# A decoder block on one core: gates and first products on GpSimd's queue, one load for keys and queries, operand sums started earlier

## The chip, the cores and the metric

The kernel runs on one core of one Trainium2 chip. The metric is the device time of one execution in microseconds (us), the median of several runs. Engines are called PE (TensorE), DVE (VectorE), ACT (ScalarE), POOL (GpSimd) and SP (SyncE, which only issues transfers here).

## The reference

```python
# x (1, 2048, 1024), all float32; D_RNN = D_ATTN = 1024, 8 heads of 128
shift, scale, gate = adaLN(c)
h = rms_norm(x) * (1 + scale) + shift
# one projection of h by W_in (1024 x 8192), its columns being
# [rnn x | rnn silu-gate | q | k | v | attn silu-gate | merge gate rnn | merge gate attn]
A = rg_lru(causal_depthwise_conv(xr)) * silu(zr)   # recurrent branch -> W -> 1024 columns
B = dilated_attention_mixture(rope(q), rope(k), v) * silu(za)
    # three causal (window, dilation) sets: (128, 1), (512, 4), (2048, 16)
merged = sigmoid(gr) * (A @ W_rnn) + sigmoid(ga) * (B @ W_attn)
out = rms_norm(x + gate * (merged @ W_out))
```

## The kernel before

Every product is fp32 accuracy made of three fp32r matmuls: an operand is split into a high part (ACT, `hi_act`) and a low part (its difference to the high part, DVE or POOL, `lo_dve`, `lo_pool`; their lines are 159, 168 and 165), and `mm3` (line 151) issues high·high, low·high, high·low. A matmul has 128 rows of weights and 512 columns.

The program goes through four stages. First the input projection, in two halves f of 1024 positions (0 to about 690 us, 690 to 1340). It uses a scheme of block products with sums of operands (Strassen's kind): the sums B11, B12, ..., T1 to T4 are made by `build_odd`, a generator that first builds the odd blocks in four steps and then makes their sums in eight half-units (lines 609 to 619), each of five DVE operations and the ACT splits `T<-hx`, `T<-t`. `values_half` interleaves that generator with the products for v (`wide_values`), whose PSUM tiles W, X, V, X, Z ... ACT evicts into `ev` (line 855) and SP stores. `issue_after(last_ev[0])` holds the next two half-units, and all behind them, until the last eviction so far. At the very start `idle_matmuls(n)` and `fill=` put matmuls on a constant (`W<-busy`) between the few real ones.

Then attention, head by head, half f by half f: `load_kq` brings keys and queries of head h and residue c into `kraw` (4 buffers), `split_kq` splits them into KQ. Between the attention's matmuls stand those of the two merged branch projections, as a generator of 64 tiles t ("pj", 24 matmuls each, eight steps k of three). For a tile, `split_y` makes the halves yh, yl of the operand, `load_g` loads the gates (grT for the first 32 tiles; gaT and the first product mrT, made by the first 32, for the rest) into `fg` (4 buffers), `evict` multiplies the product by the gate and adds mrT on DVE (lines 1784, 1786), and `store` writes mrT or the result meT. From tile TAIL0 = 40 on (about 1881.7 us) attention is over and the tiles follow one another; the eviction then writes to a tile `R` of its own rather than into `fg`. Behind tile 63 the output projection of meT, the residual and the last norm end the program.

The order on each engine is the order of the program text, run by generators at fixed steps; the transfers go out in the order of the engine that issues them, and a waiting transfer holds what stands behind it on that engine. In the tail the lines are

```python
if k == 0 and t == TAIL0:
    load_g(t)
if k == 7:
    store(t - 1)
    if t + 1 < len(tiles):
        load_g(t + 1)
```

Of the kernel before, what the change touches and what calls it, by code (L numbers as in the profile page):

```python
# [90 lines left out]
def decoder_block(ctx, tc, x, c, positions, g_norm, w_mod, b_mod, w_in, b_gate, conv_w, conv_b,  # L91
# [12 lines left out]


    vN = scratch("vN", [H, 4, NB * P, P])
    qT = scratch("qT", [D, 4, NB * P])
    kT = scratch("kT", [D, 4, NB * P])
    zaT = scratch("zaT", [D, S])
    grT = scratch("grT", [D, S])  # L110
    gaT = scratch("gaT", [D, S])
# [590 lines left out]
    with tc.manual_schedule():  # L702
        warm = T(vx, [P, 1], F32, "warm", bufs=1)
        nc.scalar.activation(warm[:], ones[:], AF.Sigmoid)
        idle_matmuls(16)
        pc = T(pg, [P, CH], F32, "pg")
        nc.tensor.transpose(pc[:, :KT], prow[:KT, :], ident[:KT, :KT])
        cc = T(vx, [P, KT], F32, "cc")
        nc.vector.tensor_copy(cc[:], pc[:, :KT])
        operand("B11")  # L710
        operand("B21")
        raws = {}
        for j in range(4):
            load_mod(j)
            for k in (2 * j, 2 * j + 1):
                if k < NRAW:
                    raws[k] = load_wide_raw(0, k)
        norm = [T(vx, [P, 3, 2], F32, "ss", bufs=4) for _ in range(2)]

        def squares(i):  # L720
            for n in range(2):
                jk = T(vx, [P, D], BF16, "hf", bufs=2)
                nc.scalar.activation(jk[:], x0[2 * i + n], AF.Square, accum_out=norm[i][:, 0, n : n + 1])

        def scale_act(r):
            nc.scalar.activation(x0[r], x0[r], AF.Copy, scale=norm[r // 2][:, 1, r % 2 : r % 2 + 1])

        def scale_dve(r):
            nc.vector.tensor_scalar(x0[r], x0[r], norm[r // 2][:, 1, r % 2 : r % 2 + 1], None, ALU.mult)

        squares(0)
        nc.scalar.activation(ca[:], cc[:], AF.Sigmoid)
        nc.vector.tensor_tensor(ca[:], ca[:], cc[:], ALU.mult)
        rstd_first(norm[0])
        squares(1)
        idle_matmuls(8)
        pt = T(pg, [P, CH], F32, "pg")
        nc.tensor.transpose(pt[:, :N_PAR], prow[:N_PAR, :], ident[:N_PAR, :N_PAR])
        nc.vector.tensor_copy(par[:], pt[:, :N_PAR])
        rstd_last(norm[0])  # L740
        scale_dve(1)
        sums(0, 1)
        rstd_first(norm[1])
        scale_act(0)
        sums(0, 1)
        rstd_last(norm[1])
        scale_act(2)
        scale_dve(3)
        ws = [wide_tiles() for kh in range(2)]
        even = ("B11", "B21")  # L750

        def products(k, js=range(KH)):
            wide_products(pv0, even, ws[k // KH], (k,), js, first=k == 0, last=k == KT - 1, lows_last=k % 2 == 0)

        def hi_k(k):
            hi_act(ws[k // KH][k % KH // 2][0][:, k % 2], raws[k][:])

        def lo_k(k):
            h, l = ws[k // KH][k % KH // 2]
            lo_dve(l[:, k % 2], raws.pop(k)[:], h[:, k % 2])  # L760
            n = k + NRAW
            if n < KT + KH:
                raws[n] = load_wide_raw(n // KT, n % KT)

        idle_matmuls(6)
        column_sums(0, 0, fill=2)
        hi_k(0)
        sums(0)
        column_sums(0, 1, fill=2)
        lo_k(0)  # L770
        turn_x(0)
        idle_matmuls(2)
        last_sums(0, fill=1)
        modulation(0)
        hi_k(1)
        sums(1, 2)
        build_x(0)
        lo_k(1)
        turn_x(1)
        pv0 = [pj_tile([P, CH]) for j in range(KH)]  # L780
        products(0)
        sums(1, 1)
        build_x(1)
        hi_k(2)
        sums(1, 2)
        lo_k(2)
        sums(1)
        turn_x(2)
        for j in range(1, 4):
            k = 2 * j  # L790
            if j == 2:
                x1 = load_x(hp, 1, "T", 14)
            products(k - 1, (0,))
            for kk in range(2):
                column_sums(j, kk)
            products(k - 1, (1, 2))
            last_sums(j)
            if j < 3:
                sums(j + 1, 1)
            modulation(j)  # L800
            products(k - 1, (3,))
            hi_k(k + 1)
            turn_x(k + 1)
            if j < 3:
                sums(j + 1, 1)
            build_x(k)
            lo_k(k + 1)
            products(k)
            if j < 3:
                hi_k(k + 2)  # L810
                sums(j + 1, 2)
            build_x(k + 1)
            if j < 3:
                sums(j + 1, 1)
                lo_k(k + 2)
                sums(j + 1)
                turn_x(k + 2)
        products(KT - 1)
        ws1 = wide_tiles()
        for k in range(KH):  # L820
            split_wide(ws1, k, raws.pop(KT + k))
# [52 lines left out]
    def values_half(f, xs):  # L874
# [16 lines left out]
        for ws in wide_values(vx, 1, n0, (0, 1), None if f else ws1):  # L891
            next(odd)
        for x, _ in enumerate(wide_values(vx, 1, n1, (1, 0), ws)):
            if x == 0:
                next(odd)
        with tc.issue_after(last_ev[0]):
            next(odd)
            next(odd)
        for x, _ in enumerate(wide_values(vx, 0, n1, (0, 1))):
            next(odd, None)  # L900
            if x == 0:
                next(odd, None)
        assert next(odd, None) is None

    xtail = T(cp, [P, 8, 3], F32, "xtail")
# [214 lines left out]
    plain_at = [None]  # L1120
    pu = [None]
    NT0, NT1 = (4, 5), 3
    QK = ((2 * D, qT, -SCALE), (3 * D, kT, 1.0))

    def scaled(t, ps, u, qs):

# [8 lines left out]

    def rotated_pairs(qp, f, Ct, St):

        for base, dstT, qs in QK:
            def rotated(i, j, ps, u, dstT=dstT, qs=qs):
                n = 2 * f + j  # L1140
                cq = slice(j * CH, (j + 1) * CH)
                t0 = T(qp, [P, CH], F32, "t0", bufs=NT0[f])
# [14 lines left out]
                def store():  # L1157
                    for hh in range(4):
                        r0 = (4 * i + hh) * P
                        nc.sync.dma_start(dstT[r0 : r0 + 32, :, n * P : (n + 1) * P],  # L1160
                                          v[0][hh * 32 : (hh + 1) * 32, :].rearrange("p (r j) -> p r j", r=4))


# [16 lines left out]

    def plain_pairs(f):

        for base, dstT, qs in QK:
            for t in range(0, 6, 2):
                def plain(i, j, ps, u, t=t, dstT=dstT, qs=qs):
                    n = 2 * f + j
                    t0 = plain_at[0]()
                    wait = scaled(t0, ps, u, qs)

                    def store():  # L1190
                        for p0, r0, m in cuts[t + i]:
                            nc.sync.dma_start(dstT[r0 : r0 + m, :, n * P : (n + 1) * P],
                                              t0[p0 : p0 + m, :].rearrange("p (r j) -> p r j", r=4))

                    steps_after(n_prod[0], ((wait + 1, store),))
# [224 lines left out]
    class Head:  # L1420
        def __init__(self, f, h):
            self.f, self.h, self.bk = f, h, banks(f)
            self.nk = (self.bk[1] + 1) * P
            self.Q1, self.V, self.V1, self.u, self.raw = {}, {}, {}, {}, {}


        def load_kq(self, c):
            rows = slice(self.h * P, (self.h + 1) * P)
            t = T(ap_, [P, KQW], F32, "kraw", bufs=4)
            q0 = self.bk[0] * P  # L1430
            queue = nc.scalar if self.f == self.h == 0 and c == 3 else nc.sync
            queue.dma_start(t[:, : self.nk], kT[rows, c, : self.nk])
            queue.dma_start(t[:, self.nk : self.nk + 2 * P], qT[rows, c, q0 : q0 + 2 * P])
            self.raw["kq", c] = t

        def split_kq(self, c):
# [4 lines left out]
        def window_queries(self, i):  # L1441

            t = T(ap_, [P, 2, 4, 4, 32], F32R, "q1")
            for l in range(2):
                src = KQ[:, l, :, self.nk + i * P : self.nk + (i + 1) * P].bitcast(F32)
                copy = nc.gpsimd if self.f or self.h else nc.vector
                copy.tensor_copy(t[:, l], src.rearrange("p r (b a) -> p b r a", b=4))
            self.Q1[i] = t[:].rearrange("p l b r a -> p l b (r a)")
# [45 lines left out]
        def scores_c(self, r):  # L1494
            tiles = []
            for i, n in enumerate(self.bk):
                w = (n + 1) * P
                if self.f or n == 0:
                    ps = T(sc, [P, CH], F32, "sc")
                o0 = P if n == 1 else 0  # L1500
                q = slice(self.nk + i * P, self.nk + (i + 1) * P)
                mm3(ps[:, o0 : o0 + w], KQ[:, 0, r, q], KQ[:, 1, r, q], KQ[:, 0, r, :w], KQ[:, 1, r, :w],
                    first=n != 1, last=True, skip_group_check=True)
                tiles.append((ps[:, o0 : o0 + w], w))

# [8 lines left out]

        def keys(self, l, w0, nb):

            ap = KQ[:, l, 0, w0 * 32 : w0 * 32 + 32]
            return bass.AP(ap.tensor, ap.offset, [list(ap.ap[0]), [32, nb], [KQW, 4], [1, 32]])

        def scores_w(self, i):  # L1520
# [202 lines left out]
    def steps(jobs):  # L1723
# [39 lines left out]
        def split_y(j, k):  # L1763
            if j < len(jobs):
# [1 line left out]
                w, ys, n = jobs[j]  # L1766
                t = Y0.pop((ys is yaT, n, k))
                hi_act(yh[:], t[:])
                (lo_dve if j and k % 2 or j > NB + 1 else lo_pool)(yl[:], t[:], yh[:])

        def load_g(t):
            j, m = tiles[t]
# [2 lines left out]
            G[t] = []  # L1775
            for src in (grT,) if ys is yaT else (gaT, mrT):
                g = T(fl, [P, CH], F32, "fg", bufs=4)
                nc.sync.dma_start(g[:], src[at_])
                G[t].append(g)

        def evict(t, ps):
# [7 lines left out]
        def store(t):  # L1789
            j, m = tiles[t]  # L1790
            w, ys, n = jobs[j]
            nc.sync.dma_start((mrT if ys is yaT else meT)[m * P : (m + 1) * P, n * CH : (n + 1) * CH], G.pop(t)[0][:])

        for k in range(KT):
            split_y(0, k)
# [3 lines left out]
        for t, (j, m) in enumerate(tiles):  # L1799
            ps = T(pj, [P, CH], F32, "pj")  # L1800
            for k in range(KT):
# [18 lines left out]
                else:  # L1820
                    if k == 0 and t == TAIL0:
                        load_g(t)
                    if k == 7:
                        store(t - 1)
                        if t + 1 < len(tiles):
                            load_g(t + 1)
# [375 lines left out]
```

## Time and profile before

| | |
|---|---|
| runs of before (us) | 2179.24, 2180.11, 2183.70; median 2180.11 |
| profiled execution | 2180.94 us, span 2179.2 us |
| busy, share of the span | PE 98%, DVE 68%, ACT 60%, POOL 49% |
| mean granted clock of TensorE | 0.997 |
| bytes moved by DMA | 522.98 MB, mean 240 GB/s |

In the rows of a timeline the first number is the start in us from the start of the span, the second the time that the row takes (matmuls of one kind that follow each other stand in one row; the end of the last is modelled), then engine, line of the kernel, operation, and out<-in by the names of tiles; brackets hold the idle time of the engine before it and what ended it. SPq, ACTq and POOL with DMA_DIRECT2D are issues of transfers. Rows of windows give start:end and length, then the busy time of an engine with its count for each engine asked for, then the granted clock of TensorE, the busy share of the 16 DMA engines and GB/s. In the part of the page on groups a row ends with the idle time before the group and what ended it.

### The profile page before, as it was taken

Reading aid. Unit: us, or ns where it says so; the run is one execution under the profiler, and the core shown is the slowest. Engines: PE = TensorE matmul, PEld = TensorE weight load, DVE = VectorE, ACT = ScalarE, POOL = GpSimd, SP = SyncE. Lnnn points to the kernel's source line nnn. Section 1 sums busy time; section 2 is a strip of 40 time slices with the busy share of each in tenths; the row PEclk is TensorE's granted clock in tenths of the full one; section 3 lists DMA queues with packets and bytes.
Section 4 is the critical chain, followed back from the end, with each engine's and each line's share of the span. In section 5 each row is a group of like instructions: output and inputs, shape, how many; then the busy total and the mean of one; then the engine's idle time right before and its main releaser. Section 6 shows DMA issues by size and latency. Waiting matters only on the chain.

```text
span 2179.2 us, 32758 instructions
## 1 busy us (share of the span) xinstructions
PE 2145.1 (98%) x10564; PEld 1791.9 (82%) x10564; DVE 1483.5 (68%) x2564; ACT 1313.1 (60%) x2621; POOL 1075.2 (49%) x803
## 2 busy tenths in 40 slices
PE   9999999999999999999999999999999999999998
PEld 6878888888788888888888887888888988878886
DVE  6579877868656535545446584577777777688887
ACT  5648668668644537457447532677888887343333
POOL 1357677667666323223224665456666665200543
PEclk9999999999999999999999999999999999999999
DMA  8457887887655378899996666888887877898552
GB/s 302 141 202 255 281 299 270 288 287 240 174 112 164 110 247 284 291 312 310 322 330 214 164 160 194 287 251 253 279 262 222 259 236 239 291 314 296 179 174 107
DMA packets 426608, 522.98 MB, mean 240 GB/s; under 512 B 104166, under 2 KB 291778, under 8 KB 425412
## 3 DMA queue, kind: packets, MB, share of 16 engines
q1 hardware_dynamic: 391860, 421.06, 61.9%
q10 hardware_dynamic: 34384, 99.78, 12.3%
q8 instruction: 84, 1.38, 0.2%
q14 instruction: 88, 0.72, 0.1%
q0 software_dynamic: 192, 0.05, 0.0%
HBM read 332.02 MB, written 188.75 MB: 239 GB/s over the span
## 4 chain that ended last, share of the span: by engine, by line
PE 59%; DMA 6%; issue 2%; POOL 2%; ACT 2%; DVE 2%; SPq 1%; ACTq 0%; POOLq 0%; DVEq 0%
PE X L151 12%; PE V L151 11%; PE pj L151 10%; PE Z L151 6%; PE W L151 6%; PE Y L151 5%; PE o L151 3%; PE sc L151 3%; DMA S<-wD 1%; PE pg L151 1%; DMA kraw<-kT 1%; PE pT L1570 1%; DMA vraw<-vN 1%; PE pT L1583 1%; DMA R<-yaT 1%
## 5 line engine op out<-in xcount | busy, mean ns | idle before, releaser
L165 POOL TENSOR_TENSOR S<-R,S 128x512 fp32r<-128x512 f32 x192 | 293.2, 1535 | 182.6 <-ACT S L159 89.3
L151 PE MATMUL X<-T,S 128*128 128x512 f32 x1344 | 326.2, 392 | 4.7 <-ACT ev L855 3.6
L151 PE MATMUL pj<-yh,S 128*128 128x512 f32 x896 | 324.5, 403 | 2.3 <-DMA S<-wD 1.6
L151 PE MATMUL V<-T,S 128*128 128x512 f32 x1344 | 324.2, 390 | 0.2 <-DVE ev L454 0.2
L151 PEld LDWEIGHTS X<-T,S 128*128 128x128 f32 x1344 | 253.3, 189 | 59.2 <-ACT ev L855 4.0
L151 PEld LDWEIGHTS V<-T,S 128*128 128x128 f32 x1344 | 252.0, 188 | 53.8 <-DVE ev L454 0.7
L165 POOL TENSOR_TENSOR S<-s,S 128x512 fp32r<-128x512 f32 x116 | 172.2, 1484 | 144.9 <-ACT S L159 105.5
L151 PEld LDWEIGHTS pj<-yh,S 128*128 128x128 f32 x896 | 168.4, 188 | 32.6 <-DVE st L1485 2.0
L151 PE MATMUL pj<-yl,S 128*128 128x512 f32 x448 | 176.2, 393 | 1.9 <-POOL yl L165 1.4
L1486 ACT ACTIVATE pp<-pp,st 128x256 f32<-128x256 f32 (+3 forms) x256 | 133.5, 523 | 52.9 <-DVE st L1485 52.3
L159 ACT ACTIVATE S<-s 128x512 fp32r<-128x512 f32 x124 | 77.4, 624 | 142.7 <-DVE s L284 92.0
L151 PE MATMUL Z<-T,S 128*128 128x512 f32 x672 | 162.0, 390 | 0.0
L151 PE MATMUL Y<-T,S 128*128 128x512 f32 x672 | 161.8, 390 | 0.0
L151 PE MATMUL W<-T,S 128*128 128x512 f32 x672 | 161.6, 389 | 0.0
L159 ACT ACTIVATE S<-R 128x512 fp32r<-128x512 f32 x200 | 121.2, 621 | 60.1 <-issue 20.4
L168 DVE TENSOR_TENSOR ptl<-pT,pth 128x384 fp32r<-128x384 f32 (+1 forms) x160 | 97.8, 628 | 77.3 <-ACT pth L159 75.1
L151 PEld LDWEIGHTS W<-T,S 128*128 128x128 f32 x672 | 126.0, 188 | 26.9 <-issue 0.9
L151 PEld LDWEIGHTS Z<-T,S 128*128 128x128 f32 x672 | 126.1, 188 | 26.2
L151 PEld LDWEIGHTS Y<-T,S 128*128 128x128 f32 x672 | 125.9, 188 | 26.1
L974 DVE SCALAR_TENSOR_TENSOR xc<-xr,par,xc 128x512 f32<-128x512 f32 x96 | 103.6, 1079 | 54.9 <-ACT xc L968 52.7
L165 POOL TENSOR_TENSOR s<-R,s 128x512 fp32r<-128x512 f32 x32 | 44.1, 1378 | 187.8 <-ACT s L159 168.7
L1550 ACT ACTIVATE pp<-pp,M 128x256 f32<-128x256 f32 (+3 forms) x256 | 118.0, 523 | 9.6 <-DVE M L1673 9.6
(417 smaller groups left out, 4902.9 us busy)
## 6 DMA issues: line engine op xcount, KB each, us to landing
sD<-S ACTq DMA_DIRECT2D x140, 512.0 KB, 3.6
S<-sD SPq DMA_DIRECT2D x140, 512.0 KB, 5.0
S<-wD SPq DMA_DIRECT2D x82, 512.0 KB, 5.6
R<-in_w_in_dram SPq DMA_DIRECT2D x144, 256.0 KB, 3.6
wD<-s ACTq DMA_DIRECT2D x64, 256.0 KB, 5.1
T<-in_w_mod_dram SPq DMA_DIRECT2D x16, 512.0 KB, 8.9
vN<-ev SPq DMA_DIRECT2D x32, 256.0 KB, 2.7
zaT<-ev SPq DMA_DIRECT2D x32, 256.0 KB, 4.4
```

The lines of the kernel that those rows point to most:

```text
L151: nc.tensor.matmul(o, lhsT=l, rhs=r, start=st, stop=sp, **kw)
L159: nc.scalar.activation(o, i, AF.Copy)
L165: nc.gpsimd.tensor_tensor(o, i, h.bitcast(F32), ALU.subtract)
L168: return nc.vector.tensor_tensor(o, i, h.bitcast(F32), ALU.subtract).ins
L974: nc.vector.scalar_tensor_tensor(xc, xr[:, i : i + CH], cw(i), xc, ALU.mult, ALU.add)
L1486: nc.scalar.activation(pdst, pdst, AF.Exp, bias=m_, scale=-1.0, accum_out=l_)
L1550: nc.scalar.activation(pp, pp, AF.Copy, scale=w)
L1570: nc.tensor.transpose(pt[:, c0 + j * P : c0 + (j + 1) * P], pp[i][:, k * P : (k + 1) * P], ident)
L1583: nc.tensor.transpose(pt[:, c * P : (c + 1) * P], pp[:, half * P : (half + 1) * P], ident)
```

## The change

It has five parts.

1. Keys and queries share one scratch tensor kqT, laid out so that a head's keys and queries for one half f lie next to each other; `load_kq` issues one transfer instead of two. For the first head three of the four go out on ACT's queue (before, one did).
2. At the start two and three idle matmuls and one fill more.
3. `values_half` calls the generator of the operand sums four times, where it called it once, while the tiles of the odd bank's first products run, and once per step after `issue_after` instead of twice first.
4. For the first tiles' operand, yl of k = 6 and 7 is made by DVE, not POOL.
5. From tile 40 on the gates and first products are loaded on POOL's queue, the results from tile 39 on are stored on it too, and both happen at step k = 2 instead of k = 7.

```diff
-    qT = scratch("qT", [D, 4, NB * P])
-    kT = scratch("kT", [D, 4, NB * P])
+    kqT = scratch("kqT", [D, 4, 2 * NB * P])
+    q_column = lambda n: (n if n < 2 else NB + n) * P
+    k_column = lambda n: (2 + n) * P
...
         turn_x(0)
-        idle_matmuls(2)
-        last_sums(0, fill=1)
+        idle_matmuls(4)
+        last_sums(0, fill=2)
...
         turn_x(1)
+        idle_matmuls(3)
...
         for x, _ in enumerate(wide_values(vx, 1, n1, (1, 0), ws)):
-            if x == 0:
+            for _ in range((1, 2, 1, 0)[x]):
                 next(odd)
         with tc.issue_after(last_ev[0]):
             next(odd)
             next(odd)
-        for x, _ in enumerate(wide_values(vx, 0, n1, (0, 1))):
+        for _ in wide_values(vx, 0, n1, (0, 1)):
             next(odd, None)
-            if x == 0:
-                next(odd, None)
...
+            self.q0, self.k0 = (self.nk, 0) if f else (0, 2 * P)
...
-            q0 = self.bk[0] * P
-            queue = nc.scalar if self.f == self.h == 0 and c == 3 else nc.sync
-            queue.dma_start(t[:, : self.nk], kT[rows, c, : self.nk])
-            queue.dma_start(t[:, self.nk : self.nk + 2 * P], qT[rows, c, q0 : q0 + 2 * P])
+            c0, w = self.f * 2 * P, self.nk + 2 * P
+            (nc.scalar if self.f == self.h == 0 and c else nc.sync).dma_start(t[:, :w], kqT[rows, c, c0 : c0 + w])
...
-                (lo_dve if j and k % 2 or j > NB + 1 else lo_pool)(yl[:], t[:], yh[:])
+                (lo_dve if (k % 2 if j else k > 5) or j > NB + 1 else lo_pool)(yl[:], t[:], yh[:])
...
-                nc.sync.dma_start(g[:], src[at_])
+                (nc.gpsimd if t >= TAIL0 else nc.sync).dma_start(g[:], src[at_])
...
-            nc.sync.dma_start((mrT if ys is yaT else meT)[...], G.pop(t)[0][:])
+            (nc.gpsimd if t >= TAIL0 - 1 else nc.sync).dma_start((mrT if ys is yaT else meT)[...], G.pop(t)[0][:])
...
-                    if k == 7:
+                    if k == 2:
                         store(t - 1)
                         if t + 1 < len(tiles):
                             load_g(t + 1)
```

The queries and keys that the attention reads out of KQ move with the offsets q0 and k0; nothing else of it changes. Three places show how instructions move. Line numbers of the changed kernel are up to two higher or lower.

The first is ACT's order at the end of the first half's products for v: `ev` are the last four evictions, `T` splits of operand sums, `S` splits of weights. Before:

```order
L159 ACTIVATE T_894<-t_197_1115 128x512
L159 ACTIVATE S_228_1262<-R_218_1236 128x512
L159 ACTIVATE S_226_1256<-s_219_1238 128x512
L855 ACTIVATE ev_1178<-W_1024 128x512
L159 ACTIVATE T_888<-hx_687 128x512
L855 ACTIVATE ev_1187<-X_1025 128x512
L159 ACTIVATE T_890<-hx_691 128x512
L855 ACTIVATE ev_1196<-V_1026 128x512
L855 ACTIVATE ev_1205<-X_1027 128x512
L159 ACTIVATE T_894<-t_211_1211 128x512
```

And in the changed kernel:

```order
L160 ACTIVATE T_902<-t_200_1139 128x512
L279 DMA sD<-S_223_1254 128x1024
L160 ACTIVATE S_229_1270<-R_219_1244 128x512
L160 ACTIVATE S_227_1264<-s_220_1246 128x512
L857 ACTIVATE ev_1194<-W_1056 128x512
L857 ACTIVATE ev_1203<-X_1057 128x512
L857 ACTIVATE ev_1212<-V_1058 128x512
L857 ACTIVATE ev_1221<-X_1059 128x512
L160 ACTIVATE S_231_1290<-R_218_1242 128x512
```

All splits T of this stage now stand ahead of the four evictions, which follow one another.

The second is SP's order at the start of attention, with the loads of the first head (`kraw`), of weights (`S<-wD`) and of a gate. Before:

```order
L1432 DMA kraw_12128<-kT 128x256
L1433 DMA kraw_12128<-qT 128x256
L1432 DMA kraw_12131<-kT 128x256
L1433 DMA kraw_12131<-qT 128x256
L1432 DMA kraw_12134<-kT 128x256
L1433 DMA kraw_12134<-qT 128x256
L339 DMA S_2258_12149<-wD 128x1024
L339 DMA S_2260_12168<-wD 128x1024
```

And in the changed kernel:

```order
L1395 DMA msk_12088<-in_cst_dram 128x896
L1432 DMA kraw_12136<-kqT 128x512
L340 DMA S_2259_12153<-wD 128x1024
L340 DMA S_2261_12172<-wD 128x1024
L1778 DMA fg_12183<-grT 128x512
```

Five issues have left SP's queue ahead of the weights; three are on ACT's.

The third is POOL's order where the tail begins, at tile 40. Before:

```order
L1687 TENSOR_TENSOR zt_19118<-zt_19118,yw_19284 128x2x256
L165 TENSOR_TENSOR yl_19530<-R_3766_19363,yh_19529 128x512
L165 TENSOR_TENSOR yl_19550<-R_3783_19451,yh_19549 128x512
L165 TENSOR_TENSOR yl_19586<-kraw_19066,yh_19585 128x512
L165 TENSOR_TENSOR st_4003_20731<-s_4002_20720,st_4003_20731 128x512
```

And in the changed kernel:

```order
L1687 TENSOR_TENSOR zt_19062<-zt_19062,yw_19228 128x2x256
L1778 DMA fg_19501<-gaT 128x512
L166 TENSOR_TENSOR yl_19474<-R_3767_19307,yh_19473 128x512
L166 TENSOR_TENSOR yl_19494<-R_3784_19395,yh_19493 128x512
L1778 DMA fg_19503<-mrT 128x512
L1792 DMA meT<-fg_19430 128x512
L1778 DMA fg_19520<-gaT 128x512
L1778 DMA fg_19522<-mrT 128x512
L166 TENSOR_TENSOR yl_19535<-kraw_19010,yh_19534 128x512
L1792 DMA meT<-R_3832_19572 128x512
```

Four transfers now stand between the second and the third yl of tile 40's operand, and three for each tile follow.

More of the change, by code (lines that the diff above doesn't have):

```diff
@@ L1122, in decoder_block @@
     NT0, NT1 = (4, 5), 3
-    QK = ((2 * D, qT, -SCALE), (3 * D, kT, 1.0))
+    QK = ((2 * D, q_column, -SCALE), (3 * D, k_column, 1.0))
     def scaled(t, ps, u, qs):
@@ L1136, in rotated_pairs, with rotated @@
     def rotated_pairs(qp, f, Ct, St):
-        for base, dstT, qs in QK:
-            def rotated(i, j, ps, u, dstT=dstT, qs=qs):
+        for base, column, qs in QK:
+            def rotated(i, j, ps, u, column=column, qs=qs):
                 n = 2 * f + j
@@ L1159, in store @@
                         r0 = (4 * i + hh) * P
-                        nc.sync.dma_start(dstT[r0 : r0 + 32, :, n * P : (n + 1) * P],
+                        nc.sync.dma_start(kqT[r0 : r0 + 32, :, column(n) : column(n) + P],
                                           v[0][hh * 32 : (hh + 1) * 32, :].rearrange("p (r j) -> p r j", r=4))
@@ L1181, in plain_pairs, with plain @@
     def plain_pairs(f):
-        for base, dstT, qs in QK:
+        for base, column, qs in QK:
             for t in range(0, 6, 2):
-                def plain(i, j, ps, u, t=t, dstT=dstT, qs=qs):
+                def plain(i, j, ps, u, t=t, column=column, qs=qs):
                     n = 2 * f + j
@@ L1191, in store @@
                         for p0, r0, m in cuts[t + i]:
-                            nc.sync.dma_start(dstT[r0 : r0 + m, :, n * P : (n + 1) * P],
+                            nc.sync.dma_start(kqT[r0 : r0 + m, :, column(n) : column(n) + P],
                                               t0[p0 : p0 + m, :].rearrange("p (r j) -> p r j", r=4))
@@ L1444, in window_queries @@
             for l in range(2):
-                src = KQ[:, l, :, self.nk + i * P : self.nk + (i + 1) * P].bitcast(F32)
+                src = KQ[:, l, :, self.q0 + i * P : self.q0 + (i + 1) * P].bitcast(F32)
                 copy = nc.gpsimd if self.f or self.h else nc.vector
@@ L1500, in scores_c @@
                 o0 = P if n == 1 else 0
-                q = slice(self.nk + i * P, self.nk + (i + 1) * P)
-                mm3(ps[:, o0 : o0 + w], KQ[:, 0, r, q], KQ[:, 1, r, q], KQ[:, 0, r, :w], KQ[:, 1, r, :w],
+                q = slice(self.q0 + i * P, self.q0 + (i + 1) * P)
+                ks = slice(self.k0, self.k0 + w)
+                mm3(ps[:, o0 : o0 + w], KQ[:, 0, r, q], KQ[:, 1, r, q], KQ[:, 0, r, ks], KQ[:, 1, r, ks],
                     first=n != 1, last=True, skip_group_check=True)
@@ L1515, in keys @@
         def keys(self, l, w0, nb):
-            ap = KQ[:, l, 0, w0 * 32 : w0 * 32 + 32]
+            ap = KQ[:, l, 0, self.k0 + w0 * 32 : self.k0 + w0 * 32 + 32]
             return bass.AP(ap.tensor, ap.offset, [list(ap.ap[0]), [32, nb], [KQW, 4], [1, 32]])
@@ L1791, in store @@
             w, ys, n = jobs[j]
-            nc.sync.dma_start((mrT if ys is yaT else meT)[m * P : (m + 1) * P, n * CH : (n + 1) * CH], G.pop(t)[0][:])
+            (nc.gpsimd if t >= TAIL0 - 1 else nc.sync).dma_start((mrT if ys is yaT else meT)[m * P : (m + 1) * P, n * CH : (n + 1) * CH], G.pop(t)[0][:])
         for k in range(KT):
```

## The prediction

> **What bounds the kernel now.** I read the page first, then TensorE's timeline at every place where its matmuls do not follow each other, then the engine that each of these stalls names.
>
> ```profile
> span 2179.2 us, 32758 instructions
> PE 2145.1 (98%) x10564; PEld 1791.9 (82%) x10564; DVE 1483.5 (68%) x2564; ACT 1313.1 (60%) x2621; POOL 1075.2 (49%) x803
> 0.00:50.00 50.00, 46.48 (x238) 0.97 0.94 320
> 100.00:150.00 50.00, 46.41 (x194) 0.93 0.63 199
> 1300.00:1936.00 636.00, 621.32 (x3781) 1.00 0.80 253
> 1936.00:2168.00 232.00, 232.00 (x1026) 1.00 0.61 205
> ```
>
> TensorE (PE) works 98% of the span, so a change can win only where it stands idle or runs at a lower clock. The windows (length, PE's busy time, granted clock, share of the DMA engines) say where that is: 3.5 us in the first 50, 3.6 us and a clock of 0.93 around 128 us, 14.7 us in attention and the start of the tail, nothing in the last 232 us. The change has a part at each of the first three places. The profiled execution took 2180.94 us, the median of the runs is 2180.11: I add my sum to the median; the profiled execution lies 0.83 us above it.
>
> **Operand sums moved ahead (around 128 us).** TensorE's, then ScalarE's (ACT), then VectorE's (DVE) timeline:
>
> ```profile
> 122.67 1.52 PE L151 MATMUL X<-S,T 128*128 128x512 f32 x6
> 127.77 5.49 PE L151 MATMUL X<-T,S 128*128 128x512 f32 x12 [3.59 <-ACT ev L855]
> 126.40:129.80 3.40, 2.03 (x5) 1.65 (x6) 3.37 (x3) 2.23 (x4) 2.98 (x2) 0.50 0.41 129
> 129.80:133.20 3.40, 3.40 (x10) 2.63 (x9) 2.50 (x5) 1.71 (x4) 0.00 (x0) 0.50 0.45 147
> 124.57 0.57 ACT L855 ACTIVATE ev<-W 128x512 f32<-128x512 f32 x1
> 126.60 0.63 ACT L159 ACTIVATE T<-hx 128x512 fp32r<-128x512 f32 x1 [1.46 <-DVE hx L612]
> 127.14 0.58 ACT L855 ACTIVATE ev<-X 128x512 f32<-128x512 f32 x1
> 105.67 0.69 DVE L168 TENSOR_TENSOR T<-hx,T 128x512 fp32r<-128x512 f32 x1 [19.04 <-ACT T L159]
> 117.93 1.78 DVE L612 TENSOR_TENSOR hx<-hx,T 128x512 f32<-128x512 f32 x1
> ```
>
> Six matmuls start 1.36 us apart in a steady row (122.67 to where the next would start, 124.03), that is 0.227 us each. So TensorE lost 127.77 − 124.03 = 3.74 us waiting for ACT's eviction ev<-X, and then had half the clock (0.50) in both windows: the twelve matmuls took from 127.77 to about 133.06, 5.3 us in place of 12 × 0.227 = 2.7, another 2.6. Together 6.3 us. ACT was late because the split T<-hx stands ahead of that eviction and waits for DVE's operand sums; DVE had stood idle for 19.04 us before 105.67 for the code holds two of these half-units, and with them all behind, until after the last eviction of the tiles before. The change starts three of the eight half-units ahead of that point, fifteen DVE operations and their ACT splits, at 0.69 us each some 10 us of DVE's work that now lies in its 19 us of idle time; on ACT the last four evictions stand together with no split between. I estimate the eviction at about 122.2 (DVE's chain ends some 5 us sooner), before 124.03. Stall and half clock go: **−6.3**. Bounds: −3 if the sums come only so much sooner that the wait, but not the clock, is halved; −6.5. What is late next in this stage is the second ev<-X, which waits for a store to free its buffer; TensorE needs that bank two tiles (5.4 us) later. In the second half of the projections the same code has a small cover, and I put half a microsecond there on the other side: **+0.4**, by no row.
>
> **The start.** Seven more idle matmuls and one more filler are meant for the clock.
>
> ```profile
> 20.00:24.00 4.00, 4.00 (x11) 0.57 1.08 362
> 38.26 0.63 ACT L159 ACTIVATE S<-R 128x512 fp32r<-128x512 f32 x1 [4.74 <-DMA R<-in_w_in_dram]
> ```
>
> At half clock eight matmuls took 0.427 in place of 0.227 us, 1.6 us. But the DMA engines are full there (1.08), and ACT still waits 4.74 us for a weight at 38.26: time won at 22 us is waited for at 38. **−0.3**, bounds −1.3 and +0.2 (one more filler in a row that ends on the sums).
>
> **Start of attention.** Here stands a stall of each kind that two parts of the change touch:
>
> ```profile
> 1347.62 5.04 POOL L165 TENSOR_TENSOR yl<-T,yh 128x512 fp32r<-128x512 f32 x4
> 1351.47 0.50 PE L151 MATMUL pj<-yl,S 128*128 128x512 f32 x1 [0.27 <-POOL yl L165]
> 1352.71 0.50 PE L151 MATMUL pj<-yl,S 128*128 128x512 f32 x1 [0.28 <-POOL yl L165]
> 1358.14 0.85 PE L151 MATMUL sc<-kq 128*128 128x128 f32 x5 [0.40 <-DVE kq L168]
> 1361.97 0.47 PE L151 MATMUL pj<-yh,S 128*128 128x512 f32 x1 [1.59 <-DMA S<-wD]
> 1352.68 0.32 SPq L1432 DMA_DIRECT2D kraw<-kT  x1
> 1356.36 0.80 SPq L339 DMA_DIRECT2D S<-wD  x2
> ```
>
> GpSimd (POOL) makes the low parts yl of the first tile one after another, 1.26 us each, and TensorE catches up with it; the load of the second kraw waits until 1352.68 for a tile that POOL's last yl frees, and the weights S<-wD stand behind it on SP, issued at 1356.36, landed after TensorE wanted them. Now the last two low parts are DVE's, which is idle here, head 0's other loads are on ACT's queue, which has nothing to do for 10 us, and the weight loads stand right behind the first kraw. The idle times are 0.27 + 0.28 + 0.40 + 1.59 = 2.5 us; counted from start to start, as above, 3.4. **−3.4**, bounds −1.5 (the weights still late) and −3.6. In the rest of attention 63 issues fewer on SP: I take **−0.8**, bounds −3 and +1, since stalls there name DVE and POOL, not SP.
>
> **First tail steps: the gates.**
>
> ```profile
> 1890.35 0.50 PE L151 MATMUL pj<-yh,S 128*128 128x512 f32 x1 [0.69 <-ACT S L159]
> 1910.88 0.73 PE L151 MATMUL pj<-yh,st 128*128 128x512 f32 x2 [0.44 <-DVE st L168]
> 1928.83 0.73 PE L151 MATMUL pj<-yh,st 128*128 128x512 f32 x2 [1.35 <-DVE st L168]
> 1934.37 0.50 PE L151 MATMUL pj<-yl,st 128*128 128x512 f32 x1 [0.71 <-DVE yl L168]
> 1925.35 0.69 DVE L1784 TENSOR_TENSOR R<-pj,fg 128x512 f32<-128x512 f32 x1 [2.19 <-DMA fg<-gaT]
> 1926.88 0.69 DVE L1786 TENSOR_TENSOR R<-R,fg 128x512 f32<-128x512 f32 x1 [0.84 <-DMA fg<-mrT]
> ```
>
> DVE waits 2.19 + 0.84 us for two gates, and 2 us later TensorE waits 1.35 us for a split that stands behind them on DVE. The four stalls of this stretch are 0.69 + 0.44 + 1.35 + 0.71 = 3.2 us idle, 3.85 from start to start. Gates issued five steps (5 × 0.68 = 3.4 us) sooner cover 2.19 + 0.84. **−3.3**, bounds −1.5 and −3.85.
>
> **The new wait.** The stores and gates are now in POOL's order, and a low part that TensorE needs stands behind them:
>
> ```profile
> 1881.37 1.30 POOL L165 TENSOR_TENSOR yl<-kraw,yh 128x512 fp32r<-128x512 f32 x1
> 1882.86 0.69 DVE L1786 TENSOR_TENSOR fg<-fg,fg 128x512 f32<-128x512 f32 x1
> 1883.58 0.32 SPq L1778 DMA_DIRECT2D fg<-mrT  x1
> 1887.55 0.74 SPq L1792 DMA_DIRECT2D meT<-fg  x1
> 1891.65 0.32 SPq L1778 DMA_DIRECT2D fg<-mrT  x1
> 1886.32 0.39 PE L151 MATMUL pj<-yl,S 128*128 128x512 f32 x1
> 1.30 0.71 POOL L642 DMA_DIRECT2D prow<-in_b_mod_dram  x1 [0.46 <-issue]
> 4.03 0.52 POOL L642 DMA_DIRECT2D prow<-in_lam_dram  x1
> L165 POOL TENSOR_TENSOR st<-s,st 128x512 fp32r<-128x512 f32 x8 | 11.3, 1416 | 134.8 <-ACT st L159 134.8
> DMA to landing us min/median/max: 2.8/5.2/10.9
> ```
>
> Before, POOL made this yl at 1881.37, and TensorE used it at 1886.32, 5 us later. Now four transfers stand ahead of it: mrT of tile 40, free only after the eviction of tile 39 (1882.86 + 0.69 = 1883.55; SP issued it at 1883.58), the store of tile 39, gaT of tile 41, and mrT of tile 41, whose buffer is the source of that store. On SP this last one waited from the store at 1887.55 to 1891.65, 4.1 us. So on POOL: 1883.58, an issue of 0.7, the store from 1884.3, landed at 1888.4, the last issue 0.65, the yl 1.30, ready at 1890.35: TensorE waits 1890.35 − 1886.32 = 4.0 us. An issue of 0.65 is an estimate between the rows of 0.52 and 0.71 us, for shorter transfers. As that is longer than the 3.74 us that cost half the clock at 128 us, I add the same 2.6: **+6.6**. Bounds from the landing times of meT: 2.8 gives a stall of 2.7 without the clock, 10.9 gives 10.8 + 2.6 = 13.4. The Trainium skill ("TensorE: Matmul & The Clock Gate", What's actually happening) has the clock halved after an idle window of about 3.4 us that runs freely, so a stall of 4.0 holds a whole window only if it starts at the right moment; by that rule the sum would have +4.0 here in most phases. The trace has half clock after 3.59 us of idle time and none after 1.59, which agrees.
>
> In the steady tail POOL is all but idle (the last row: from 1935 us on, 134.8 us before eight operations); three issues of 0.65 are 2 us in a tile of 24 × 0.227 = 5.45, and gates issued by 3.8 us after a tile's start land 5.2 later, at 9.0, needed at 11.2. Nothing for that.
>
> The sum: −6.3 + 0.4 − 0.3 − 3.4 − 0.8 − 3.3 + 6.6 = **−7.1**: 2180.11 − 7.1 = **2173.0**.
>
> **Rivals.**
> *The new wait is short* (no half clock, landing 2.8 to 4.1): 2.6 to 3.9 us less, 2169.1 to 2170.4. For it: the row of landings; against: the same wait took 4.1 on SP. 16%.
> *The stall at 128 us stays or goes elsewhere*, DVE's chain being slowed (its 128x512 operations take 1.78 us there when POOL works too), or the new wait has the longest landing: 2173.0 + 6.3 = 2179.3, or 2173.0 + 6.8 = 2179.8, no difference that can be told. 22%.
> *POOL's issues are slow, and the gates fall behind.* No row shows POOL issuing a transfer of 128 rows beside a busy DVE. The point from which it decides is 5.45 / 3 = 1.8 us an issue, beyond which three no longer fit in a tile; at 2.0 each of 23 tiles takes 0.55 us more, 12.7 us: 2185.7, slower; at 3.0 it would be 2255. Against: rows of 0.52 to 0.71 and DVE's tail work, whose operations of 0.68 us show no contention. The Trainium skill ("SBUF — State Buffer", two separate sides) warns that GpSimd cannot write its descriptors while DVE runs certain copies, and says that operations of two inputs are not among them; no run here shows it. 12%. Both this far end of the new wait and the stall at 128 us left in place: 2186.1, 5%.
>
> **How the numbers follow.** Forecast 45%. Some 0.2% (4.4 us) is what a measurement can tell from no change. Faster by more: 45 + 16 = 61%; same: 22%; slower: 12 + 5 = 17%. The range reaches from 2167.5 (the short wait, and the other gains at their far bounds) to 2181.5 (the second rival and the noise of the median); it leaves out the slower cases.
>
> **What would show it.** Right: no PE stall on ACT ev at 128 us and a clock of 1.00 there; S<-wD issued before 1354; no DVE wait on fg beyond 0.5 us after 1900; one PE wait on POOL yl of about 4 us near 1880, with half clock behind it. Wrong: POOL issues above 1 us, PE waits spread over the tail, or the wait at 128 us turned over to DVE.

## The result, and the profile after

The changed kernel took 2188.58 us (median, 2187.92 to 2190.71) against 2180.26 before: a ratio of 1.0038 (1.0027 to 1.0049), 8.3 us slower, where 7.1 faster was forecast. The page and the windows of its profile:

```profile
span 2186.8 us, 32665 instructions
PE 2146.7 (98%) x10571; PEld 1792.1 (82%) x10571; DVE 1486.6 (68%) x2566; ACT 1311.8 (60%) x2621; POOL 1112.4 (51%) x874
0.00:50.00 50.00, 46.62 (x245) 1.00 0.94 320
100.00:150.00 50.00, 49.64 (x218) 1.00 0.64 202
1300.00:1936.00 636.00, 615.47 (x3747) 0.99 0.79 249
```

The stage at 128 us is mended (49.64 busy and full clock, against 46.41 and 0.93). The window of attention and the tail's start is worse: 20.5 us without a matmul where there were 14.7. To compare stages I use one measure, worked out from all matmuls of a profile: from the start of each to the start of the next, less what that takes in a steady row (0.227 us for 512 columns, less for narrower ones). Half clock is in it. In us:

| stage (us from the start) | before | after | forecast of the change | measured |
|---|---|---|---|---|
| 0 to 50 | 8.0 | 6.4, and seven more matmuls of 0.227 | −0.3 | 0.0 |
| 100 to 150 (operand sums) | 6.5 | 0.7 | −6.3 | −5.8 |
| 150 to 450 | 1.1 | 4.7 | none | +3.6 |
| 550 to 800 | 3.4 | 3.8 | +0.4 | +0.4 |
| 1300 to 1400 (start of attention) | 5.6 | 8.2 | −3.4 | +2.6 |
| 1400 to 1850 | 22.6 | 22.3 | −0.8 | −0.3 |
| 1850 to 2000 (tail) | 4.9 | 12.0 | −3.3 + 6.6 | +7.1 |

The last column adds up to 7.6 us, the difference of the two spans. Nearly all of the tail's loss is one wait. GpSimd's (POOL's) timeline, then TensorE's (PE's) row, then SP's rows:

```profile
1883.95 0.56 POOL L1778 DMA_DIRECT2D fg<-mrT  x1 [2.18 <-DVE fg L1786]
1884.51 0.54 POOL L1792 DMA_DIRECT2D meT<-fg  x1
1887.51 0.54 POOL L1778 DMA_DIRECT2D fg<-gaT  x1 [2.45 <-DMA meT<-fg]
1892.53 0.54 POOL L1778 DMA_DIRECT2D fg<-mrT  x1 [4.48 <-DMA meT<-fg]
1893.08 1.27 POOL L166 TENSOR_TENSOR yl<-kraw,yh 128x512 fp32r<-128x512 f32 x1
1894.41 0.79 PE L152 MATMUL pj<-yl,S 128*128 128x512 f32 x1 [8.29 <-POOL yl L166]
1879.53 1.08 SPq L1792 DMA_DIRECT2D meT<-fg  x1
1883.24 0.67 SPq L1928 DMA_DIRECT2D st<-in_w_o_dram  x1
```

The chain is the forecast's: mrT of tile 40, the store of tile 39, gaT and mrT of tile 41, then the yl that TensorE waits for. But gaT waited until 1887.51 for the store of tile 38 that SP had issued at 1879.53, 8.0 us; and the last mrT until 1892.53 for the store issued at 1884.51, again 8.0 us (the profile puts its landing 7.7 us after the issue). From start to start TensorE lost 8.45 us, and 1.9 us more at half clock until 1898.5.

At the start of attention TensorE's, ACT's and SP's rows say what took the place of the four stalls before:

```profile
1349.22 0.50 PE L152 MATMUL pj<-yl,S 128*128 128x512 f32 x1 [0.69 <-POOL yl L166]
1358.53 0.50 PE L152 MATMUL pj<-yh,S 128*128 128x512 f32 x1 [0.67 <-DVE fg L1784]
1361.64 2.45 PE L152 MATMUL sc<-kq,q 128*128 128x128 f32 x12 [2.14 <-DVE q L1446]
1349.20 1.92 ACTq L1432 DMA_DIRECT2D kraw<-kqT  x3
1359.80 0.63 ACT L160 ACTIVATE kq<-kraw 128x512 fp32r<-128x512 f32 x1 [0.85 <-DMA kraw<-kqT]
1348.60 3.11 SPq L340 DMA_DIRECT2D S<-wD  x2
1352.00:1358.00 6.00, 5.75 (x28) 4.33 (x26) 1.52 (x3) 1.26 (x2) 0.00 (x0) 1.00 1.02 395
```

The weights S<-wD, which TensorE had waited for, go out at 1348.60, ahead of three of the first head's loads (1349.20). In the window behind it the DMA engines are full (1.02, 395 GB/s). So the weights are there, and the last part of keys and queries is split only at 1359.80, after which DVE makes q and TensorE has waited 2.14 us.

### The profile page after: what moved, and what is told of

Its sections match the earlier page's. It is cut to its first block, busy times and chain, and to the rows that moved or that the text cites. A ratio compares the mean times of both kernels' runs of the same rounds, so it can differ in the third digit from the quotient of the medians.

```text
span 2186.8 us, 32665 instructions
## 1 busy us (share of the span) xinstructions
PE 2146.7 (98%) x10571; PEld 1792.1 (82%) x10571; DVE 1486.6 (68%) x2566; ACT 1311.8 (60%) x2621; POOL 1112.4 (51%) x874
## 3 DMA queue, kind: packets, MB, share of 16 engines
q10 hardware_dynamic: 34528, 100.30, 12.3%
## 4 chain that ended last, share of the span: by engine, by line
PE 55%; DMA 7%; POOL 4%; DVE 3%; issue 3%; ACT 1%; SPq 1%; ACTq 0%; POOLq 0%; DVEq 0%
PE X L152 11%; PE V L152 11%; PE pj L152 8%; PE Z L152 6%; PE W L152 6%; PE Y L152 5%; PE o L152 3%; PE sc L152 3%; POOL kq L166 1%; DMA vraw<-vN 1%; PE pg L152 1%; PE pT L1570 1%; DMA kraw<-kqT 1%; POOL yl L166 1%; DMA fg<-gaT 1%
```

## The experiments

All ratios are to the kernel before, run beside it on the same chip. Stages are given by the measure above. My theory after the result: the loss is the one wait on GpSimd's order, plus the order of loads at the start of attention; the rivals are named in each expectation.

**e1, part 5 alone.** The kernel before with the two queues and the step of the tail:

```diff
-                nc.sync.dma_start(g[:], src[at_])
+                (nc.gpsimd if t >= TAIL0 else nc.sync).dma_start(g[:], src[at_])
...
-            nc.sync.dma_start((mrT if ys is yaT else meT)[...], G.pop(t)[0][:])
+            (nc.gpsimd if t >= TAIL0 - 1 else nc.sync).dma_start((mrT if ys is yaT else meT)[...], G.pop(t)[0][:])
...
-                    if k == 7:
+                    if k == 2:
                         store(t - 1)
```

> The kernel before with part 5 alone (gates, first products and stores of the tail on GpSimd's queue, at step k = 2). Theory (the yl of k = 6 in tile 40 stands on GpSimd behind two transfers that wait for stores to land): one TensorE wait of 8 us or more on POOL yl near 1890 and about 2 us of half clock, less the 3 to 4 us of small DVE waits in tiles 40 to 49 that go: 2180.3 + 8.4 + 2 - 3.5 = 2187. Rival A (the loss of the whole change comes from the start of attention and the stage behind 150 us): no slower than before, 2177 to 2181. Rival B (GpSimd's issues cost more in every tile): a loss spread over the tail, no single wait above 3 us.

2188.36 us, 1.0040 (1.0027 to 1.0053). One wait of 8.12 us on yl, tail 12.3 us. This part alone loses all that the change loses.

**e2, the change without part 5** (the same edit, taken back).

> The changed kernel with part 5 undone (all on SP at k = 7 again). Theory: the wait on POOL yl is gone, the rest of the change remains: at the operand sums -5.8 and +3.6 given back behind 150 us, at the start of attention +2.6, small things +0.3: 2180.3 + 0.7 = 2181, so no difference from before. Rival A: the other four parts lose on their own, 2184 or more. The forecast's own terms without the new wait and without the gates: 2180.3 - 10.4 = 2170.

2179.60 us, 0.9997 (0.9989 to 1.0006): no difference. The tail is at 3.9. The other four parts together bring nothing.

**e3, tile 40's transfers after the low part**: the changed kernel with one number in one tile.

```diff
-                    if k == 2:
+                    if k == (5 if t == TAIL0 else 2):
                         store(t - 1)
```

> The changed kernel with one step moved: in tile 40 alone the store of tile 39 and the gates of tile 41 are issued at k = 5 instead of k = 2, so that GpSimd makes the yl of k = 6 ahead of them. Theory: the one long wait goes, 8.4 us and 2 us of clock, and the rest of the tail keeps its gain: 2188.6 - 10.4 = 2178, at most 2180 if tile 41's gates are now late. Rival B (GpSimd's issues cost in every tile): gains at most 3, 2185 or more.

2179.95 us, 0.9997 (0.9988 to 1.0006), 8.6 us less than the changed kernel from one number in one tile. The tail is at 3.0. GpSimd's issues in every tile cost nothing that shows.

**e4, part 3 alone**: before, with `values_half` of the change.

```diff
-            if x == 0:
+            for _ in range((1, 2, 1, 0)[x]):
                 next(odd)
...
-        for x, _ in enumerate(wide_values(vx, 0, n1, (0, 1))):
+        for _ in wide_values(vx, 0, n1, (0, 1)):
             next(odd, None)
-            if x == 0:
-                next(odd, None)
```

> The kernel before with part 3 alone (operand sums started earlier). Theory: the wait and the half clock at 128 us go, -5.8, and 3.6 is given back between 150 and 250 us because the later work of ACT and GpSimd does not move with TensorE: 2178. Rival (the loss behind 150 us belongs to another part, the start): -5.8 in full, 2174.5.

2177.76 us, 0.9988 (0.9980 to 0.9997). The stage at 128 us goes from 6.5 to 0.5, the one from 150 to 450 stands at 3.6. Part 3 pays, about 2.5 us. The rival falls: the start is as before here, and the stage behind 150 us is still above the 1.1 of before.

**e5, part 1 alone**: before, with `kqT` and

```diff
+            (nc.scalar if self.f == self.h == 0 and c else nc.sync).dma_start(t[:, :w], kqT[rows, c, c0 : c0 + w])
```

> The kernel before with part 1 alone (one load for keys and queries, three of the first head's four on ACT's queue). Theory (at the start of attention the DMA engines are full, and the weights S<-wD, which now stand ahead of the first head's loads, land first, so that the keys and queries land later): the wait of 1.8 us for the weights goes, a wait of TensorE of 2 to 4 us for kq or q of the first head comes in its place: excess between 1300 and 1400 of 7 to 9 us against 5.6 before, 2180.3 + 2 = 2182. The forecast: the same excess 2 to 3 us lower, 2178.

2183.45 us, 1.0016 (1.0008 to 1.0025). The start of attention is at 8.8, with the wait that the changed kernel shows. TensorE's timeline:

```profile
1362.11 0.50 PE L152 MATMUL pj<-yh,S 128*128 128x512 f32 x1 [0.96 <-DVE fg L1785]
1365.23 1.78 PE L152 MATMUL sc<-kq,q 128*128 128x128 f32 x12 [2.15 <-DVE q L1447]
```

**e6, part 4 alone.**

```diff
-                (lo_dve if j and k % 2 or j > NB + 1 else lo_pool)(yl[:], t[:], yh[:])
+                (lo_dve if (k % 2 if j else k > 5) or j > NB + 1 else lo_pool)(yl[:], t[:], yh[:])
```

> The kernel before with part 4 alone (yl of k = 6 and 7 of the first tile on DVE). Theory: the tile that holds up the second kraw load is free 2 us sooner, the loads and the weights behind them on SP go out sooner in the same order as before: the two waits on POOL yl go or turn into one (DVE and GpSimd slow each other: 1.70 and 1.25 us an operation in the changed kernel), excess between 1300 and 1400 of 3.5 to 5, 2179. Rival (part 4 is what spoils the start of attention): 7 or more, 2182.

2180.32 us, 1.0001 (0.9992 to 1.0009): neutral, start of attention at 4.8. The move saves less than two operations: beside DVE's two, GpSimd's two take 3.43 us together, 1.72 each, where all four took it 5.04, 1.26 each. (Of the two figures in the expectation, 1.70 is GpSimd's and 1.25 DVE's.)

**e7, the step alone**: before, with `k == 2` in place of `k == 7`, all on SP.

> The kernel before with the tail's store and gates at step k = 2, but still on SP's queue. Theory (it is GpSimd's order that carries the wait to TensorE; on SP the same waits for stores to land, 8 us and more, hold only loads of weights): no wait on POOL yl; the weights S<-wR and st behind it come later, which may cost 0 to 3 us: 2180 to 2183. Rival (the step alone does it): 2186 or more.

2186.11 us, 1.0028 (1.0018 to 1.0038). My theory was wrong here: without GpSimd's queue the step still loses 6 us. There is no wait on yl, but SP's, DVE's and TensorE's rows show that the early transfers now hold up something else:

```profile
1886.51 0.43 SPq L1792 DMA_DIRECT2D meT<-fg  x1
1892.35 0.32 SPq L1778 DMA_DIRECT2D fg<-mrT  x1
1893.67 0.42 SPq L2137 DMA_DIRECT2D st<-gateD  x1
1891.64 0.68 DVE L1784 TENSOR_TENSOR R<-pj,fg 128x512 f32<-128x512 f32 x1
1900.22 1.29 DVE L1932 TENSOR_TENSOR st<-st,st 128x512 f32<-128x512 f32 x2 [5.97 <-DMA st<-gateD]
1902.26 0.47 PE L151 MATMUL pj<-yh,S 128*128 128x512 f32 x1 [2.49 <-DVE R L1784]
```

The load of mrT for tile 41 holds SP until 1892.35. The profile names what ended this wait: not a store, but DVE's eviction of tile 40 (R, done at 1892.32). The loads for the output projection stand behind it: gateD goes out at 1893.67 (1886.80 before), DVE waits 5.97 us for it and, being in order, evicts the next tile late. So the early step costs some 6 us on either queue. On GpSimd the landing of a store comes into the path, on SP an eviction; the queue decides what is waited for and who pays.

**e8, e3 with the first head's loads back on SP, ahead of the weights.**

```diff
-            (nc.scalar if self.f == self.h == 0 and c else nc.sync).dma_start(...)
+            (nc.scalar if self.f == self.h == 0 and c == 3 else nc.sync).dma_start(...)
```

> The kernel of e3 with the first head's loads of c = 1 and 2 back on SP, ahead of the weights as before (one load each, yl of k = 6 and 7 on DVE). Theory: the keys and queries land first again, excess between 1300 and 1400 falls from 8.5 to 4 or 5: 2179.9 - 4 = 2176. Rival (it is the single, longer load that is slow, not its place): no change, 2180.

2176.08 us, 0.9981 (0.9972 to 0.9989): the time that was expected, 3.9 us less than e3. The profiles do not show it in one place: the start of attention fell only from 8.5 to 6.9; the tail fell from 3.0 to 0.8 and the stage behind 150 us from 5.7 to 3.9, which this edit does not touch. A single profile of a stage scatters by about 2 us. ACT's and TensorE's rows:

```profile
1355.62 0.63 ACT L160 ACTIVATE kq<-kraw 128x512 fp32r<-128x512 f32 x1 [10.09 <-DMA kraw<-kqT]
1356.97 1.82 ACT L160 ACTIVATE kq<-kraw 128x512 fp32r<-128x512 f32 x3 [0.73 <-DMA kraw<-kqT]
1356.30 0.33 PE L152 MATMUL sc<-kq 128*128 128x128 f32 x1 [1.25 <-ACT kq L160]
```

All four parts are now split by 1358.8 and the wait for q is gone, but the first comes later, and TensorE waits for that.

**e9, the changed kernel without mrT for tile 41** (its result lacks that addend).

```diff
-            for src in (grT,) if ys is yaT else (gaT, mrT):
+            for src in (grT,) if ys is yaT else (gaT,) if t == TAIL0 + 1 else (gaT, mrT):
```

> The changed kernel without the load of the first product (mrT) for tile 41 alone, and without its addition (that tile's result lacks it). GpSimd's order then has one transfer less ahead of the yl of k = 6, the one that waited until 1892.53 for the store of tile 39. Theory (the wait is the landing of stores, one after the other): the yl is made when gaT of tile 41 is out, at 1888.05 + 1.27 = 1889.3; TensorE waits 3.4 us instead of 8.4, about 2188.4 - 5 = 2183, 2181.5 if the half clock goes too. Rival (GpSimd's issues or its queue are slow as such): the wait shrinks by one issue, 0.6 us.

2181.56 us, 1.0009 (1.0000 to 1.0018); the wait, in TensorE's timeline:

```profile
1887.32 0.50 PE L152 MATMUL pj<-yl,S 128*128 128x512 f32 x1 [3.66 <-POOL yl L166]
```

3.8 us from start to start instead of 8.45: leaving out one issue of 0.54 us takes 4.6 us from the wait. It is the landing that the transfer waits for. The half clock behind the wait stays.

**e10, part 2 alone.**

```diff
-        idle_matmuls(2)
-        last_sums(0, fill=1)
+        idle_matmuls(4)
+        last_sums(0, fill=2)
...
         turn_x(1)
+        idle_matmuls(3)
```

> The kernel before with part 2 alone (seven idle matmuls and a fill more at the start). Theory: clock 1.00 from 20 to 24 us, excess of the first 50 us lower by 1.5 and seven matmuls of 0.227 us more: no difference, 2179.5 to 2180.5. Rival (the time won at 22 us is kept): 2178.4.

2180.45 us, 1.0003 (0.9993 to 1.0012). The first 50 us are at 7.0 instead of 8.0, plus seven matmuls of 0.227: nothing.

**e11, parts 3 and 5 with tile 40 at k = 5**, parts 1, 2 and 4 left out.

> The kernel before with part 3 and with part 5, tile 40's store and gates at k = 5; parts 1, 2 and 4 left out. Theory (parts 1, 2 and 4 pay nothing or cost): excess between 1300 and 1400 back to 5.5 from 6.9 in e8, the tail as there: 2176.1 - 1.5 = 2174.5. Rival (e8's gain needs the single load or the low parts on DVE): 2177.5 or more.

2175.26 us, 0.9978 (0.9969 to 0.9988). Start of attention at 4.6, tail at 1.6.

**e12, the same with the single load, on the queues of before** (part 1 as in e8).

> e8 without parts 2 and 4: the single load for keys and queries with SP's queue as before, part 3, and part 5 with tile 40 at k = 5. Theory (the single load with its place kept is neutral): as e11 within 1 us, 2174 to 2176. Rival (part 4 gave e8 its gain): 2177 or more.

2174.84 us, 0.9979 (0.9970 to 0.9987): 5 us faster than before and not to be told from e11. Its start of attention is at 4.5, against 6.9 in e8. That part 4 makes this difference is not shown: the times of e8 and e12 agree within their intervals, and the stage scatters by more between profiles of the same instructions (below).

**e13, three loads behind the low part**: the changed kernel with two loads of in_w_o and one of gateD on GpSimd's queue, where they stand behind the yl.

```diff
-        (nc.scalar if k else nc.sync).dma_start(t[:], w_o[...])
+        (nc.scalar if k else nc.gpsimd).dma_start(t[:], w_o[...])
...
-            nc.sync.dma_start(v["gate"][:], gateD[0:1, :].broadcast_to([P, D]))
+            nc.gpsimd.dma_start(v["gate"][:], gateD[0:1, :].broadcast_to([P, D]))
```

> The changed kernel with three loads of the output projection (two of in_w_o, one of gateD, 512 KB each, issued on SP between 1883.2 and 1886.3) put on GpSimd's queue, where they stand behind the yl of k = 6. Theory (the stores of tiles 38 and 39 take 8 us to land because SP, no longer held by the stores and gates, sends these loads 2 to 3 us sooner and fills the DMA engines): the store of tile 39 lands in 4 to 6 us from its issue, the wait of TensorE shrinks from 8.4 to 4.5 to 6.5 us; the loads that are now late may cost a few us further on, so the trace decides and not the time. Rival (a store beside the tail's first loads takes 8 us whatever else is sent): the wait stays within 1 us of 8.4.

2186.34 us, 1.0029 (1.0017 to 1.0042). The profiled execution was the slowest of six, 2192.11 us. GpSimd's and TensorE's rows:

```profile
1887.24 0.54 POOL L1792 DMA_DIRECT2D meT<-fg  x1
1889.45 0.54 POOL L1778 DMA_DIRECT2D fg<-gaT  x1 [1.67 <-DMA meT<-fg]
1893.24 0.54 POOL L1778 DMA_DIRECT2D fg<-mrT  x1 [3.25 <-DMA meT<-fg]
1895.12 0.79 PE L152 MATMUL pj<-yl,S 128*128 128x512 f32 x1 [6.41 <-POOL yl L166]
```

The store of tile 39 lands 6.0 us after its issue instead of 8.0, and the wait is 6.6 instead of 8.45 from start to start. So these three loads make about 2 of the 8 us: the landing that the profile gives is 5.7 us here, and 7.7, 7.4 and 7.5 in the changed kernel, e1 and e9, which keep them on SP. What makes up the rest stays open; loads of weights (wR), 256 KB each, are still in flight beside the store, and no run took them away.

## Why the prediction was wrong

The forecast was −7.1 and the two profiles differ by +7.6. Of these 14.7 us the start of attention makes 6.0, the new wait 3.7, the stage behind 150 us 3.6, and all other terms together 1.4.

*The new wait: mechanism right, size wrong.* Its place, its chain and the half clock were as written. The term was 4.0 + 2.6; it measured 8.45 + 1.9 = 10.3. The step that failed is the landing of 4.1 us, taken from "the store at 1887.55 to 1891.65". The load of 1891.65 did not wait for that store: what ended its wait is DVE's eviction of tile 40, done at 1891.61. DVE's row of before, and the landing of that store as the profile gives it (the last number, in us):

```profile
1890.93 0.68 DVE L1784 TENSOR_TENSOR R<-pj,fg 128x512 f32<-128x512 f32 x1
meT<-fg SPq DMA_DIRECT2D x1, 256.0 KB, 8.2
```

And the same store in the changed kernel:

```profile
meT<-fg POOLq DMA_DIRECT2D x1, 256.0 KB, 7.7
```

So the landing had been 8.2 us all along. In the prediction's own sum it puts the yl at 1884.3 + 8.2 + 0.65 + 1.30 = 1894.45, a wait of 8.1 and a term of 10.7; the forecast would have been 2177.1, still the wrong way. I had also written down the longest landing of meT, 10.9, and its bound of 13.4. And I passed over gaT's own wait, for the store of tile 38; e9 shows that alone it would cost 3.8. The change did not make this landing longer: the other kernels with the order of before have 7.7 to 8.2 (e2, e4, e5, e6, e10), and while the store was in flight the DMA engines were full, before and after. Windows of before, then after (the last columns are DMA share and GB/s):

```profile
1888.00:1892.00 4.00, 3.31 (x14) 1.00 0.98 384
```

```profile
1888.00:1892.00 4.00, 0.00 (x0) 0.92 1.03 402
```

*The gates: right in kind, perhaps smaller.* Without that wait the changed kernel's tail would be at 12.0 − 10.3 = 1.7, 3.2 less than before; 3.3 was the term. Over the kernels it is less, since the stage scatters: 3.2 to 5.1 with the order of before (before, e2, e4, e5, e6, e10), 0.8 to 3.0 where tile 40's step is k = 5 (e3, e8, e11, e12); the means differ by 2.3.

*The start of attention: the wrong sign.* Forecast −3.4, measured +2.6, and 3.2 for part 1 alone (8.8 in e5 against 5.6). The step that failed is "the weight loads stand right behind the first kraw", costed as a gain of 1.59 us of wait and nothing else. The stall that went was named, but what would then be late was not asked of the transfers: the DMA engines are full there, and whoever is served first makes the other late. The Trainium skill ("DMA: Bandwidth & Descriptors", Issuing engines are not separate DMA queues) says that transfers issued from several engines run on the same DMA engines and that this only saves the time of issuing. The trace agrees: the three loads from ACT's queue took a median of 8.7 us to land in the changed kernel,

```profile
kraw<-kqT ACTq DMA_DIRECT2D x3, 256.0 KB, 8.7
```

and the weights on SP landed sooner than before. Before, then after:

```profile
S<-wD SPq DMA_DIRECT2D x4, 512.0 KB, 7.3
```

```profile
S<-wD SPq DMA_DIRECT2D x4, 512.0 KB, 5.5
```

That it is the place and not the single, longer load is shown by the times: part 1 alone costs 3.6 us (e5), the single load on the queues of before costs nothing (e12 against e11), and moving the loads back gains 3.9 (e8 against e3). The stage's figures divide this no further: five profiles with the same instructions there (the changed kernel, e2, e3, e9 and e13) lie between about 6 and 9.5. The term for the rest of attention, −0.8, counted 63 issues fewer on SP; there are 65, and the stage measured −0.3, no more than scatter.

*The operand sums: right, but given back.* −5.8 of −6.3. What the forecast put at nothing is the stage behind. In the kernels with part 3 the stage from 150 to 450 us is at 3.6 to 5.9, in those without it at 1.1 to 3.0. The means differ by 2.3; the profile of before is the lowest of its kind, so the rest of the 3.6 us is scatter of single executions. e4's gain of 2.5 us fits that. TensorE's rows of the changed kernel show waits for ACT there:

```profile
219.51 3.02 PE L152 MATMUL X<-T,S 128*128 128x512 f32 x12 [0.31 <-ACT u L385]
239.86 1.43 PE L152 MATMUL X<-T,S 128*128 128x512 f32 x5 [1.01 <-ACT u L385]
```

The kernel before has none, but e5, without part 3, has the same two of 1.3 us together. That the work behind does not move with TensorE is therefore my reading, not shown; the cause of what is given back stays open.

*The start: no gain*, as argued from the DMA engines; that the matmuls added, seven with the filler's, take their own 1.6 us would have settled it.

*The rivals.* None of them was it. The slow issue on GpSimd is ruled out: 0.54 to 0.63 us each, beside a working DVE, with 2.1 to 6.2 us of idle time a tile. The longest landing came nearest, but it was priced with all other gains kept, and so ended at no change. The range left out the case that two terms fail at once; the one rival of that kind, 2186.1 at 5%, came near in time by luck: its second term, the stall at 128 us left in place, did not happen. The range's low end does not follow from its own bounds either: they add up to 2165.0, not 2167.5.

## What to carry to other kernels

The time from a transfer's issue to the next instruction of its queue is not its landing. Ask the profile what ended that instruction's wait, and read the landing itself: here 4.1 us was read where 8.2 stood on record. A landing also depends on what is in flight beside it: with three loads sent later (e13) it took 5.7 us instead of 7.7. Where the DMA engines are full, taking a wait for one load away means naming the load that is late instead. Before a transfer is moved ahead in an engine's order, look at what its buffer waits for: one number in one tile (k = 5 for k = 2) was worth 8.6 us here, and the best mix, e12, gains 5.0 of 2179.8.

## What was not expected of the hardware

GpSimd issues a transfer of 128 rows of 2 KB in 0.54 to 0.63 us, no dearer than the shorter ones at the start (0.50 to 0.71). In the changed kernel a store of 256 KB took 2.7 us to land when issued at 1898.72, with the DMA engines 51% busy, and 8.0 us when issued at 1921.46, with them full (1.02). After 8.3 us without a matmul TensorE ran 4.1 us at half clock, against 5.3 us after the 3.6 us without one in the kernel before: the longer wait did not cost more clock.
